# Contrast adjustment on one core: the third and sixth load split into 58 and 6 KB of each row, and the first and fourth store made to wait for GpSimd

## The chip, the core and the metric

The kernel runs on one core of a Trainium2 chip. The names of the profile are used for its engines: PE is TensorE (matrix multiplies), DVE is VectorE, ACT is ScalarE, POOL is GpSimd, and SP is the engine whose queue starts the transfers (DMA) between the chip's main memory (HBM) and the on-chip buffer (SBUF). The SBUF has 128 partitions; an array of 128x16384 is 16384 numbers in each of them. A started transfer is carried out by 16 DMA engines side by side. The metric is the device time of one execution in microseconds (us).

## What is computed

The input `x` holds 16 images of 3 channels, 512x512 float32 numbers each: 48 planes of 262144 pixels, 50.33 MB. The factor is 1.5.

```python
mean = np.mean(x, axis=(2, 3), keepdims=True)
return np.clip(mean + factor * (x - mean), 0, 1).astype(np.float32)
```

A plane can't be written before all of it has been read, since its mean needs every pixel. Every byte is read once and written once, 100.66 MB in all.

## The kernel before, in words

The kernel sees `x` as one line of numbers and cuts it into six tiles of 128 rows with 16384 numbers (64 KB) each, 8 planes to a tile, 16 rows to a plane. A tile is 8.39 MB. The buffer `ring` has three slots, so tile `t` uses slot `t % 3`: tiles 0, 1 and 2 come in at once, and tiles 3, 4 and 5 can be loaded only when the stores of tiles 0, 1 and 2 have emptied their slots.

All transfers are started by SP (`load`, line 77; `store`, line 80), in the order in which the program text names them, and SP does not go past one that still waits. That order, written out at the end of the kernel, is: tile 0 in three loads (2048, 6144 and 8192 columns), load 1, load 2, the stores of tile 0, 1 and 2, loads 3, 4 and 5, the stores of tile 3, 4 and 5.

`compute(t)` does the following to a tile once it has landed:

- The row sums. DVE adds up the first 4352 columns (`tensor_reduce`, line 85) and ACT the others, by a copy of them onto themselves that also writes their sum (line 89). Tile 0 is done in two halves of 8192 columns. The partial sums go into columns of `sums`.
- The mean. PE multiplies each partial sum by the constant `blockw`, which adds up the 16 rows of a plane and scales the result; the products are accumulated in `bias`, in PSUM (line 100).
- The pixels. DVE makes two passes over the tile in place: multiply by the factor and add the bias (line 103), then clip to 0 and 1 (line 106).
- The store. Tile 0 is done in two cuts: columns 0 to 2048 get both passes and a store of 1 MB, then the other 14336 columns get theirs and a store of 7 MB. All other tiles are one cut.

POOL only prepares constants and `blockw` at the start (lines 61 and 63). The waits between engines and transfers are put in by the framework from what each instruction reads and writes; the order on each engine is that of the text.

Of the kernel before, what the change touches and what calls it, by code (L numbers as in the profile page):

```python
# [1 line left out]

# [4 lines left out]


P = 128  # L10
ROW = 16384
HALF = ROW // 2
BUFS = 3
SHORT = 2048
SUM = 4352


@with_exitstack
def kernel(
    ctx: ExitStack,  # L20
    tc: tile.TileContext,
    x: bass.AP,
    factor: float,
    out: bass.AP,
):

    nc = tc.nc
    f32 = mybir.dt.float32  # L30
    Alu = mybir.AluOpType
    Act = mybir.ActivationFunctionType

    B, C, H, W = x.shape
    n_img, n_pix = B * C, H * W
    ppi = n_pix // ROW
    per_tile = P // ppi
    n_tiles = n_img // per_tile
    assert ppi * ROW == n_pix and per_tile * n_tiles == n_img

    factor = float(factor)
    wconst = (1.0 - factor) / float(n_pix)

    x_f = x.rearrange("b c h w -> (b c h w)")
    out_f = out.rearrange("b c h w -> (b c h w)")

    def dram(ap, t, c0=0, c1=ROW):
        return bass.AP(tensor=ap.tensor, offset=t * P * ROW + c0, ap=[[ROW, P], [1, c1 - c0]])

    consts = ctx.enter_context(tc.tile_pool(name="consts", bufs=1))  # L50
    xpool = ctx.enter_context(tc.tile_pool(name="xpool", bufs=1))
    small = ctx.enter_context(tc.tile_pool(name="small", bufs=1))
    psum = ctx.enter_context(tc.tile_pool(name="psum", bufs=1, space=bass.MemoryType.PSUM))


    sums = small.tile([P, 4 * n_tiles], f32, name="sums")
    bias = psum.tile([P, n_tiles], f32, name="bias")

    blockw = consts.tile([P, P], f32, name="blockw")
    blocks = blockw.rearrange("p (a b) -> p a b", b=ppi)  # L60
    nc.gpsimd.memset(blockw, wconst)  # L61
    for base, step in ((0, -ppi), (ppi - 1, ppi)):
        nc.gpsimd.affine_select(  # L63
            out=blocks,
            in_=blocks,
            compare_op=Alu.is_ge,
            fill=0.0,
            base=base,
            pattern=[[step, per_tile], [0, ppi]],
            channel_multiplier=1 if step < 0 else -1,  # L70
        )


    ring = xpool.tile([P, BUFS, ROW], f32, name="ring")

    def load(t, c0=0, c1=ROW):
        nc.sync.dma_start(out=ring[:, t % BUFS, c0:c1], in_=dram(x_f, t, c0, c1))  # L77

    def store(t, c0=0, c1=ROW):
        nc.sync.dma_start(out=dram(out_f, t, c0, c1), in_=ring[:, t % BUFS, c0:c1])  # L80

    def add(t, col, c0, c1, c2):
        xt = ring[:, t % BUFS, :]
        own = sums[:, 4 * t + col : 4 * t + col + 2]
        nc.vector.tensor_reduce(  # L85
            out=own[:, 0:1], in_=xt[:, c0:c1], axis=mybir.AxisListType.X, op=Alu.add
        )
        part = xt[:, c1:c2]
        nc.scalar.activation(out=part, in_=part, func=Act.Copy, accum_out=own[:, 1:2])  # L89
        return [own[:, 1:2], own[:, 0:1]]  # L90

    def compute(t, *cuts):
        xt = ring[:, t % BUFS, :]
        if t == 0:
            parts = add(t, 0, 0, SUM, HALF) + add(t, 2, HALF, HALF + SUM, ROW)
        else:
            parts = add(t, 0, 0, SUM, ROW)
        shift = bias[:, t : t + 1]
        for k, part in enumerate(parts):
            nc.tensor.matmul(shift, blockw, part, start=k == 0, stop=k == len(parts) - 1)  # L100
        for c0, c1 in zip((0, *cuts), (*cuts, ROW)):
            part = xt[:, c0:c1]
            nc.vector.tensor_scalar(  # L103
                out=part, in0=part, scalar1=factor, scalar2=shift, op0=Alu.mult, op1=Alu.add
            )
            nc.vector.tensor_scalar(  # L106
                out=part, in0=part, scalar1=0.0, scalar2=1.0, op0=Alu.max, op1=Alu.min
            )
            store(t, c0, c1)

    with tc.manual_schedule():
        load(0, 0, SHORT)
        load(0, SHORT, HALF)
        load(0, HALF, ROW)
        load(1)
        load(2)
        compute(0, SHORT)
        compute(1)
        compute(2)
        load(3)  # L120
        load(4)
        load(5)
        compute(3)
        compute(4)
        compute(5)


# [1 line left out]
_INS = ['x', 'factor']  # L129
_OUTS = [((16, 3, 512, 512), 'float32')]  # L130

_NUMBERS = {'factor': 1.5}


# [26 lines left out]
```

## Time and profile before

| what | value |
|---|---|
| time, median of 3 runs (lowest, highest) | 239.5 us (239.36, 239.76) |
| profiled execution, first to last instruction (span) | 237.3 us |
| bytes moved, mean rate over the span | 100.66 MB, 424 GB/s |
| DVE busy / ACT busy / POOL busy | 137.4 / 59.9 / 1.1 us |

The profiled execution is one run of its own, and its record gives the span only; no time of its own that would take in what lies around the span. The median of the runs is 2.2 us above that span.

In the timeline each row gives the start of an instruction in us from the start of the span, its duration, the engine, the line of the kernel, the operation, what it writes and reads, how many are merged in the row, and in brackets how long the engine sat idle before and what ended that. A table by stretches of time gives for each stretch the busy time of each engine and, in the last two columns, the mean busy share of the 16 DMA engines and the rate at which they moved bytes; a packet is counted where it starts, so a share can exceed 1. The rows of the DMA queue are its packets, their bytes, and the time that they took as a share of 16 engines' span.

### The profile page before, as it was taken

To read this page: it belongs to the slowest core of one execution; us is meant where nothing else is said; L and a number is where in the kernel's file an instruction comes from. 1 tells how busy PE (TensorE), PEld (TensorE's weight loads), DVE (VectorE), ACT (ScalarE), POOL (GpSimd) and SP (SyncE) were. 2 spreads that over 40 slices of the span, in tenths; PEclk is the share of its full clock that TensorE was granted. 3 is DMA by queue.
4 is the path that set the end of the run, shared out by engine and by line. 5 is a ranking of instruction groups with operands and counts; after the bars stand their busy time and mean duration, and the time that the engine had idled before them with its cause. 6 is when DMAs were issued, how large, how long until landed. Compare 5 with 4: busy or idle time off the path is not lost.

```text
span 237.3 us, 186 instructions
## 1 busy us (share of the span) xinstructions
PE 7.9 (3%) x28; PEld 6.9 (3%) x28; DVE 137.4 (58%) x21; ACT 59.9 (25%) x15; POOL 1.1 (0%) x7
## 2 busy tenths in 40 slices
PE   0010100010001000000000000100000000000000
PEld 0010100010001000000000000100000000000000
DVE  0071899949998998000000043499989998991000
ACT  2051300980492000000000049319509800000000
POOL 1000000000000000000000000000000000000000
DMA  7999989899799798989899998989899998989894
GB/s 289 418 442 442 530 353 530 353 486 398 331 464 454 341 530 353 530 353 519 365 442 442 398 486 353 530 354 530 353 475 409 431 453 376 508 353 530 353 530 177
DMA packets 2160, 100.66 MB, mean 424 GB/s; under 512 B 240, under 2 KB 240, under 8 KB 240
## 3 DMA queue, kind: packets, MB, share of 16 engines
q1 hardware_dynamic: 2160, 100.66, 98.7%
HBM read 50.33 MB, written 50.33 MB: 424 GB/s over the span
## 4 chain that ended last, share of the span: by engine, by line
DVE 43%; DMA 36%; ACT 9%; PE 2%; SPq 1%; issue 0%; DVEq 0%; ACTq 0%
DMA ring<-in_x_dram 36%; DVE ring L103 18%; DVE ring L106 18%; ACT ring L89 9%; DVE sums L85 6%; PE bias L100 2%; SPq L77 1%; SPq L80 0%; DVEq L103 0%; ACTq L89 0%
## 5 line engine op out<-in xcount | busy, mean ns | idle before, releaser
L89 ACT ACTIVATE ring<-ring 128x12032 f32<-128x12032 f32 (+1 forms) x7 | 58.0, 8280 | 128.2 <-DMA ring<-in_x_dram 128.2
L85 DVE TENSOR_REDUCE sums<-ring 128x1 f32<-128x4352 f32 x7 | 32.8, 4683 | 63.9 <-DMA ring<-in_x_dram 63.9
L103 DVE TENSOR_SCALAR ring<-ring,bias 128x16384 f32<-128x16384 f32 (+2 forms) x7 | 52.8, 7538 | 12.9 <-PE bias L100 12.9
L106 DVE TENSOR_SCALAR ring<-ring 128x16384 f32<-128x16384 f32 (+2 forms) x7 | 52.3, 7476 | 0.2
L100 PE MATMUL bias<-sums,blockw 128*128 128x1 f32 x28 | 7.9, 360 | 189.1 <-ACT ring L89 175.4
L100 PEld LDWEIGHTS bias<-sums,blockw 128*128 128x128 f32 x28 | 6.9, 314 | 190.0 <-ACT ring L89 159.4
L89 ACT ACT_TABLE_LOAD x1 | 1.3, 1283 | 0.8 <-PEq L142 0.8
L89 ACT ACTIVATION_READ_ACCUMULATOR ring<-ring 128x1 f32 x7 | 1.3, 187 | 0.0
L63 POOL TENSOR_SCALAR_AFFINE_SELECT blockw<-blockw 128x128 f32<-128x128 f32 x2 | 0.7, 340 | 0.1
L61 POOL MEMSET blockw<- 128x128 f32 x1 | 0.2, 204 | 0.3 <-POOLq L142 0.3
L142 POOL MEMSET const-bfloat16-1.0<- 128x1 bf16 x1 | 0.1, 102 | 0.0
L142 POOL MEMSET const-uint8-127<- 128x1 uint8 x1 | 0.1, 102 | 0.0
L142 POOL MEMSET const-float32-0.0<- 128x1 f32 x1 | 0.1, 98 | 0.3 <-issue 0.3
L142 POOL MEMSET const-float32-1.0<- 128x1 f32 x1 | 0.1, 98 | 0.0
## 6 DMA issues: line engine op xcount, KB each, us to landing
out_dram<-ring SPq DMA_DIRECT2D x1, 7168.0 KB, 35.9
ring<-in_x_dram SPq DMA_DIRECT2D x1, 4096.0 KB, 20.8
ring<-in_x_dram SPq DMA_DIRECT2D x1, 3072.0 KB, 11.6
ring<-in_x_dram SPq DMA_DIRECT2D x1, 1024.0 KB, 4.7
out_dram<-ring SPq DMA_DIRECT2D x1, 1024.0 KB, 34.3
ring<-in_x_dram SPq DMA_DIRECT2D x5, 57.7
out_dram<-ring SPq DMA_DIRECT2D x5, 27.0
```

Of the source, the lines that this page charges most:

```text
L61: nc.gpsimd.memset(blockw, wconst)
L63: nc.gpsimd.affine_select(out=blocks, in_=blocks, compare_op=Alu.is_ge, fill=0.0, base=base, pattern=[[step, per_tile], [0, ppi]], channel ...
L77: nc.sync.dma_start(out=ring[:, t % BUFS, c0:c1], in_=dram(x_f, t, c0, c1))
L85: nc.vector.tensor_reduce(out=own[:, 0:1], in_=xt[:, c0:c1], axis=mybir.AxisListType.X, op=Alu.add)
L89: nc.scalar.activation(out=part, in_=part, func=Act.Copy, accum_out=own[:, 1:2])
L100: nc.tensor.matmul(shift, blockw, part, start=k == 0, stop=k == len(parts) - 1)
L103: nc.vector.tensor_scalar(out=part, in0=part, scalar1=factor, scalar2=shift, op0=Alu.mult, op1=Alu.add)
L106: nc.vector.tensor_scalar(out=part, in0=part, scalar1=0.0, scalar2=1.0, op0=Alu.max, op1=Alu.min)
L142: nc = _bacc.Bacc("TRN2", target_bir_lowering=False, num_devices=1)
```

## The change

Tiles 2 and 5 come in by two loads each: columns 0 to 14848 (58 KB of each row), then the last 1536 columns (6 KB). The cut of tile 0 is gone; it gets one pass of each kind and one store, like the others. Tiles 0 and 3 have the last 32 columns clipped by POOL instead of DVE. Just ahead of that clip POOL copies column 0 of tile 2 (of tile 5) into a column of `sums`; this copy needs the 58 KB part of that tile. DVE's sum of that tile starts at column 1, and the copied column goes to PE as a third partial sum. Since the store of tile 0 (tile 3) needs the columns that POOL clips, it waits for POOL, and so for the 58 KB part.

```diff
+TAIL = 1536
+EDGE = 32
+TURNS = {2: 0, 5: 3}
...
+    def edge(t):
+        xt = ring[:, t % BUFS, :]
+        own = sums[:, 4 * t + 2 : 4 * t + 3]
+        nc.gpsimd.tensor_copy(out=own, in_=xt[:, 0:1])
+        before = ring[:, TURNS[t] % BUFS, ROW - EDGE : ROW]
+        nc.gpsimd.tensor_scalar(
+            out=before, in0=before, scalar1=0.0, scalar2=1.0, op0=Alu.max, op1=Alu.min
+        )
+        return own
...
+        elif t in TURNS:
+            parts = add(t, 0, 1, SUM, ROW) + [edges[t]]
...
-        for c0, c1 in zip((0, *cuts), (*cuts, ROW)):
-            part = xt[:, c0:c1]
-            nc.vector.tensor_scalar(
-                out=part, in0=part, scalar1=factor, scalar2=shift, op0=Alu.mult, op1=Alu.add
-            )
-            nc.vector.tensor_scalar(
-                out=part, in0=part, scalar1=0.0, scalar2=1.0, op0=Alu.max, op1=Alu.min
-            )
-            store(t, c0, c1)
+        nc.vector.tensor_scalar(
+            out=xt, in0=xt, scalar1=factor, scalar2=shift, op0=Alu.mult, op1=Alu.add
+        )
+        own = xt[:, 0 : ROW - EDGE] if t in TURNS.values() else xt
+        nc.vector.tensor_scalar(
+            out=own, in0=own, scalar1=0.0, scalar2=1.0, op0=Alu.max, op1=Alu.min
+        )
+        for later, turn in TURNS.items():
+            if turn == t:
+                edges[later] = edge(later)
+        store(t)
+
+    def load_split(t):
+        load(t, 0, ROW - TAIL)
+        load(t, ROW - TAIL, ROW)
...
-        load(2)
-        compute(0, SHORT)
+        load_split(2)
+        compute(0)
...
-        load(5)
+        load_split(5)
```

More of the change, by code (lines that the diff above doesn't have):

```diff
@@ L90, in add, with compute @@
         return [own[:, 1:2], own[:, 0:1]]
-    def compute(t, *cuts):
+    def edge(t):
[7 more added lines that the diff above has]
+        return own
+    edges = {}
+    def compute(t):
         xt = ring[:, t % BUFS, :]
```

## The prediction

> **What bounds the kernel now.** I read the busy times first, then the row of the DMA queue.
>
> ```profile
> PE 7.9 (3%) x28; PEld 6.9 (3%) x28; DVE 137.4 (58%) x21; ACT 59.9 (25%) x15; POOL 1.1 (0%) x7
> ...
> q1 hardware_dynamic: 2160, 100.66, 98.7%
> ```
>
> No engine is busy for more than 58% of the span, but the 16 DMA engines are for 98.7%. The transfers are the bound, back to back, from 1.8 us to the end. The direction turns three times: loads 0 to 2, stores 0 to 2, loads 3 to 5, stores 3 to 5. There is no slack in this chain: any stretch in which the DMA engines have nothing queued is added to the time in full, and only packets that take longer than they must can be won back.
>
> So next I looked for slow packets. In the packet records every 64 KB row takes 2.418 us on its DMA engine, reading or writing, with two places as exceptions: the last row of load 2 on each engine (mean 3.53 us, started about 58.1) and the last row of load 5 (mean 2.54). Both are the last reads ahead of stores that were already queued. The timeline shows the first one without packets, by when ACT could start on each landed tile:
>
> ```profile
> 22.58 3.40 ACT L89 ACTIVATE ring<-ring 128x3840 f32<-128x3840 f32 x1 [6.22 <-DMA ring<-in_x_dram]
> ...
> 41.93 10.23 ACT L89 ACTIVATE ring<-ring 128x12032 f32<-128x12032 f32 x1 [15.86 <-DMA ring<-in_x_dram]
> ...
> 62.40 10.23 ACT L89 ACTIVATE ring<-ring 128x12032 f32<-128x12032 f32 x1 [10.15 <-DMA ring<-in_x_dram]
> ...
> 159.21 10.23 ACT L89 ACTIVATE ring<-ring 128x12032 f32<-128x12032 f32 x1 [8.96 <-DMA ring<-in_x_dram]
> ...
> 178.57 10.23 ACT L89 ACTIVATE ring<-ring 128x12032 f32<-128x12032 f32 x1 [9.04 <-DMA ring<-in_x_dram]
> ```
>
> Load 1 came 41.93 - 22.58 = 19.35 us after load 0, load 2 20.47 us after that, load 5 19.36 us after load 4. All that can be won is therefore 3.53 - 2.42 = 1.11 us at the first turn and 0.12 us at the second, 1.2 us or 0.5%.
>
> **The change part by part.** *One store of tile 0 for two.* Eight packets of 8 KB (0.309 us) and eight of 56 KB (2.116) become eight of 64 KB (2.418): 19.40 - 19.34 = 0.06 us won, in the DMA chain. DVE's two passes over 16384 columns (8.76 + 8.70) replace 1.29 + 1.23 + 7.68 + 7.63: 0.4 us less, hidden, because line 103 of tile 1 waits for ACT's sum, which ends at 52.3.
>
> *The split loads.* From packet sizes (24 KB 0.912 us, 56 KB 2.116) a row of 58 KB costs 2.19 us and one of 6 KB 0.23, 0.01 more a row than a whole one: 0.06 us a tile, plus 0.01 for a completion. The second issue on SP (0.4 us) stands behind running transfers. On each DMA engine 8 x 0.234 = 1.87 us of reading remain behind the 58 KB part: this is the cover under which the store must get ready.
>
> *The third matmul* of tiles 2 and 5 is one of about 0.3 us on PE, and DVE's and ACT's sums barely change; the stores of these tiles are ready long before their turn (store 5 at 214.6, started after the stores of 3 and 4). Nothing.
>
> *The wait of the stores.* This decides. SP holds store 0 until POOL is done, and behind it stand stores 1 and 2 and loads 3 to 5; with load 2 through, the DMA engines have nothing else. Without the slow row load 2's 58 KB part has landed everywhere at about 41.91 + 8 x 2.191 = 59.45; load 5's at 159.12 + 17.54 = 176.66 (landings of loads 1 and 4). From POOL's end on, the store costs 0.06 us until SP issues it and 1.02 us until bytes move:
>
> ```profile
> 93.76 0.02 SPq L80
> 93.78 0.04 issue
> ```
>
> SP's first issue was at 0.80, and the table by stretches has its first packets after 1.80:
>
> ```profile
> 1.60:1.80 0.20, 0.00 (x0) 0.00 (x0) 0.00 (x0) 0.20 (x1) 0.20 (x1) 1.00 0.00 0
> 1.80:2.00 0.20, 0.00 (x0) 0.00 (x0) 0.00 (x0) 0.20 (x1) 0.02 (x1) 1.00 2.52 369
> ```
>
> *When does POOL run?* Its own rows are short, but all stand before 1.82 us, with DVE idle until 12.94:
>
> ```profile
> 0.41 0.10 POOL L142 MEMSET const-uint8-127<- 128x1 uint8 x1
> 0.80 0.20 POOL L61 MEMSET blockw<- 128x128 f32 x1 [0.29 <-POOLq L142]
> 1.07 0.75 POOL L63 TENSOR_SCALAR_AFFINE_SELECT blockw<-blockw 128x128 f32<-128x128 f32 x2
> ```
>
> At both turns DVE is in the middle of its passes:
>
> ```profile
> 53.43 8.76 DVE L103 TENSOR_SCALAR ring<-ring,bias 128x16384 f32<-128x16384 f32 x1 [3.07 <-PE bias L100]
> 62.22 8.70 DVE L106 TENSOR_SCALAR ring<-ring 128x16384 f32<-128x16384 f32 x1
> 70.83 4.68 DVE L85 TENSOR_REDUCE sums<-ring 128x1 f32<-128x4352 f32 x1
> ...
> 174.25 8.76 DVE L103 TENSOR_SCALAR ring<-ring,bias 128x16384 f32<-128x16384 f32 x1 [0.75 <-PE bias L100]
> 183.04 8.70 DVE L106 TENSOR_SCALAR ring<-ring 128x16384 f32<-128x16384 f32 x1
> 191.65 4.68 DVE L85 TENSOR_REDUCE sums<-ring 128x1 f32<-128x4352 f32 x1
> ```
>
> The trace has no POOL instruction beside a DVE one, so the wait is bounded from both sides: nothing at the low end, and at the high end until DVE leaves the pair of passes, 70.91 - 59.45 = 11.5 us and 191.74 - 176.66 = 15.1 us. One row speaks for the high end. The sum of line 85 goes through 4352 / 4.68 = 0.93 numbers per ns and partition; the passes, from two widths, (16384 - 2048) / (8.757 - 1.292) = 1.92, and they write as much as they read. [...] I take the high end, with POOL getting in only where a pass ends.
>
> [...] The trace agrees with the doubled rate (1.92 against 0.93); that POOL blocks, nothing here shows yet. [...]
>
> **The sum.** POOL has two instructions. The copy may slip between the passes, at 62.20; by then DVE's next pass is waiting and goes next, and the clip comes at its end (if the copy doesn't slip in, both come there). I allow 0.2 us for the copy and 0.34 for the clip, the rows of `blockw`. First turn: 70.91 + 0.2 + 0.34 + 0.06 + 1.02 = 72.5 us for the first bytes of store 0. Before, the last engine had read load 2 at 62.03 (packet records; the landing followed 0.35 us later), and the store went on at once: +10.5 us. Second turn: 191.74 + 0.2 + 0.34 + 0.06 + 1.02 = 193.4 against 178.13: +15.2 us (the second half of the kernel keeps its own clock, counted from load 3). The slow rows and the dearer split vanish in these gaps; the merged store gives 0.06 back. The span becomes 237.3 + 10.5 + 15.2 - 0.1 = 262.9. The runs lie 2.2 us above the span (239.5 against 237.3), which I keep: **265.1 us**. Both terms hang on DVE's rows alone; with POOL's two instructions between nothing and 1 us it is 264.0 to 266.0.
>
> **The rivals.** *POOL runs beside DVE (ends faster).* The store is then issued under the cover. First bytes at 59.45 + 0.04 + 0.2 + 0.34 + 1.08 = 61.1, load 2's data ends at 59.45 - 0.35 + 1.87 = 60.97: a gap of 0.1, and -0.9 against 62.03. Second turn: 178.3 against 178.13, +0.2. With the merged store -0.8: 238.7 us. With POOL's rows at 0.1 each there is no gap: 238.4. A store that starts from empty may pay at each turn what the first loads paid (8 KB packets of 0.6 to 1.0 us instead of 0.31), up to 0.7: 240.1. For it speak POOL's short rows; against it the doubled rate. It decides if POOL's copy starts within 1 us of the landing. Chance 0.30.
>
> *Both of POOL's instructions slip in at the first end of a pass (slower, less so).* Clip done at 62.20 + 0.54, first bytes 63.8: +1.8. Second turn: 183.01 + 0.54 + 1.08 = 184.6: +6.5. Together 8.3, 247.7 us. For it: POOL has both instructions in hand while it waits, and the gap between passes (62.20 to 62.22) exists. Against it: DVE's next pass also waits there. Chance 0.18. One turn this way and one as in the forecast gives 239.5 + 17.0 - 0.1 = 256.4 either way; chance 0.08.
>
> *The forecast*, both turns late by the pair of passes: chance 0.44.
>
> **How the numbers follow.** Two signs hold most of the chance. The forecast's own range is 264.0 to 266.0. Leaving out the fast rival would leave out 3 in 10, so the range goes from its low end, 238.4, to 265.8. A change under 0.2% (0.5 us) can't be told from none here. Of the fast rival's 0.30 I give 0.22 to faster, 0.05 to within, 0.03 to slower (it needs most of the start-up price); all other cases are slower: 0.73 together.
>
> **What would show it.** In the changed profile: POOL's copy of 128x1 and clip of 128x32 starting at the end of a line-103 or line-106 pass, or stretched over it (forecast: copy from 62.2 or 70.9, clip after 70.9); DMA slices with no share between about 61 and 72 us and again for some 15 us at the second turn; SP's store 0 waiting for POOL and not DVE. If the last rows of load 2 run at full rate, as I assume, then its 58 KB part lands near 59.5. I am wrong if POOL's two rows stand near 59.6 with their short durations beside a running pass, or if the packets of the turns are slow even with no store queued.

## The result and the profile after

The changed kernel takes 265.03 us (median of 4 runs, 264.93 to 265.32) against 239.63 us before (239.36 to 239.85). The ratio is 1.107, with a 95% interval of 1.105 to 1.109: 25.4 us slower. The forecast was 265.1 us.

The page of the changed kernel gives the same two rows that stood first in the prediction, and its DMA slices (the span in 40 slices of 6.6 us, busy share in tenths):

```profile
PE 8.7 (3%) x32; PEld 7.7 (3%) x32; DVE 137.2 (52%) x19; ACT 59.9 (23%) x15; POOL 27.6 (10%) x11
...
DMA  7999999972379998997989997999603799799977
...
q1 hardware_dynamic: 2304, 100.66, 89.0%
```

DVE and ACT work as long as before; the DMA engines have the same bytes, but their share of the span fell from 98.7% to 89.0%, and two holes stand in the slices. POOL went from 1.1 to 27.6 us with four instructions more. The table by stretches (busy us of PE, PEld, DVE, ACT and POOL, then the clock, DMA share and GB/s) shows the holes with POOL busy through both:

```profile
62.00:72.00 10.00, 0.10 (x1) 0.11 (x1) 9.96 (x3) 9.84 (x2) 9.11 (x2) 1.00 0.05 20
72.00:74.00 2.00, 0.48 (x2) 0.39 (x2) 2.00 (x1) 0.00 (x0) 0.00 (x0) 1.00 1.01 426
...
190.00:203.00 13.00, 0.58 (x2) 0.50 (x2) 12.96 (x3) 10.19 (x2) 12.99 (x2) 1.00 0.00 0
203.00:205.00 2.00, 0.00 (x0) 0.00 (x0) 2.00 (x1) 0.00 (x0) 0.00 (x0) 1.00 1.24 524
```

From the packet records the DMA engines stood idle for 11.3 us at the first turn and 14.8 at the second (means of the 16 engines): 26.1 us, about as much as the span grew (263.3 - 237.3 = 26.0). The timeline gives the reason (L118 and L122 are DVE's two passes, L98 and L100 POOL's copy and clip, L83 the stores):

```profile
53.53 8.76 DVE L118 TENSOR_SCALAR ring<-ring,bias 128x16384 f32<-128x16384 f32 x1 [3.36 <-PE bias L117]
59.62 2.72 POOL L98 COPY sums<-ring 128x1 f32<-128x1 f32 x1 [57.78 <-DMA ring<-in_x_dram]
61.52 10.23 ACT L92 ACTIVATE ring<-ring 128x12032 f32<-128x12032 f32 x1 [9.16 <-DMA ring<-in_x_dram]
62.30 8.81 POOL L100 TENSOR_SCALAR ring<-ring 128x32 f32<-128x32 f32 x1
62.32 8.73 DVE L122 TENSOR_SCALAR ring<-ring 128x16384 f32<-128x16384 f32 x1
70.97 4.67 DVE L88 TENSOR_REDUCE sums<-ring 128x1 f32<-128x4351 f32 x1
71.14 23.56 SPq L83 DMA_DIRECT2D out_dram<-ring  x3
...
185.42 8.76 DVE L118 TENSOR_SCALAR ring<-ring,bias 128x16384 f32<-128x16384 f32 x1 [0.75 <-PE bias L117]
188.03 6.19 POOL L98 COPY sums<-ring 128x1 f32<-128x1 f32 x1 [116.91 <-DMA ring<-in_x_dram]
...
194.18 8.81 POOL L100 TENSOR_SCALAR ring<-ring 128x32 f32<-128x32 f32 x1
194.21 8.72 DVE L122 TENSOR_SCALAR ring<-ring 128x16384 f32<-128x16384 f32 x1
```

The copy of one column begins when the 58 KB part has landed (59.62) and ends with the pass that is running (62.29). The clip of 32 columns begins then and ends with the next pass (71.05). Store 0 goes out at 71.14, though load 2 was complete at 61.5, as ACT's start shows. The second turn repeats it: DVE's passes there end at 194.2 and 202.9.

### The profile page after: what moved, and what is told of

Same layout as the page of the kernel before. It is cut to its first block, busy times and chain, and to the rows that moved or that the text cites. A ratio compares the mean times of both kernels' runs of the same rounds, so it can differ in the third digit from the quotient of the medians.

```text
span 263.3 us, 203 instructions
## 1 busy us (share of the span) xinstructions
PE 8.7 (3%) x32; PEld 7.7 (3%) x32; DVE 137.2 (52%) x19; ACT 59.9 (23%) x15; POOL 27.6 (10%) x11
## 5 line engine op out<-in xcount | busy, mean ns | idle before, releaser
L88 DVE TENSOR_REDUCE sums<-ring 128x1 f32<-128x4352 f32 (+1 forms) x7 | 32.8, 4680 | 74.7 <-DMA ring<-in_x_dram 74.7
L118 DVE TENSOR_SCALAR ring<-ring,bias 128x16384 f32<-128x16384 f32 x6 | 52.5, 8758 | 14.1 <-PE bias L117 14.1
L122 DVE TENSOR_SCALAR ring<-ring 128x16384 f32<-128x16384 f32 (+1 forms) x6 | 52.2, 8698 | 0.2
L98 POOL COPY sums<-ring 128x1 f32<-128x1 f32 x2 | 8.9, 4453 | 174.7 <-DMA ring<-in_x_dram 174.7
L100 POOL TENSOR_SCALAR ring<-ring 128x32 f32<-128x32 f32 x2 | 17.6, 8814 | 0.0
L117 PE MATMUL bias<-sums,blockw 128*128 128x1 f32 x32 | 8.7, 359 | 199.9 <-ACT ring L92 185.4
L117 PEld LDWEIGHTS bias<-sums,blockw 128*128 128x128 f32 x32 | 7.7, 316 | 200.8 <-ACT ring L92 169.3
```

What stands on the lines that cost most here:

```text
L88: nc.vector.tensor_reduce(out=own[:, 0:1], in_=xt[:, c0:c1], axis=mybir.AxisListType.X, op=Alu.add)
L98: nc.gpsimd.tensor_copy(out=own, in_=xt[:, 0:1])
L100: nc.gpsimd.tensor_scalar(out=before, in0=before, scalar1=0.0, scalar2=1.0, op0=Alu.max, op1=Alu.min)
L118: nc.vector.tensor_scalar(out=xt, in0=xt, scalar1=factor, scalar2=shift, op0=Alu.mult, op1=Alu.add)
L122: nc.vector.tensor_scalar(out=own, in0=own, scalar1=0.0, scalar2=1.0, op0=Alu.max, op1=Alu.min)
```

## The experiments

The theory: POOL stands still while DVE runs a pass at the doubled rate (1.92 numbers per ns and partition, against 0.93 in its sums). The rivals: the wait for a part of a load costs the time whichever engine sees it; any DVE work holds POOL; POOL waits for DVE by a semaphore of the program; POOL's two instructions are slow in themselves.

### ACT in place of POOL

```diff
-        nc.gpsimd.tensor_copy(out=own, in_=xt[:, 0:1])
+        nc.scalar.activation(out=own, in_=xt[:, 0:1], func=Act.Copy)
...
-        nc.gpsimd.tensor_scalar(
-            out=before, in0=before, scalar1=0.0, scalar2=1.0, op0=Alu.max, op1=Alu.min
-        )
+        nc.scalar.activation(out=before, in_=before, func=Act.Copy)
```

(Both stand behind ACT's sum of the tile in between, so that they don't hold it up; DVE clips all columns.)

> The copy of column 0 and the touch of the last 32 columns go from POOL to ACT, which is idle at both turns (DVE clips all columns; ACT copies the last 32 onto themselves). Same wait for the 58 KB part, same two small instructions. My theory (POOL stands still while a DVE pass at the doubled rate runs): ACT does both within 0.6 us of the landing, store 0 is issued near 60.2 and not 71.1, and the time is 238.7 us (238.4 to 240.1). Rival (the wait for a landed part costs the time, whichever engine sees it): 265 us again.

Measured: 239.19 us, ratio 0.9987 (0.9978 to 0.9997). The timeline of this run:

```profile
59.56 0.20 ACT L98 ACTIVATE sums<-ring 128x1 f32<-128x1 f32 x1 [7.23 <-DMA ring<-in_x_dram]
59.67 0.21 ACT L100 ACTIVATE ring<-ring 128x32 f32<-128x32 f32 x1
59.91 34.73 SPq L83 DMA_DIRECT2D out_dram<-ring  x3
```

The wait, the split and the order of the transfers are those of the changed kernel, and the 25 us are gone; store 0 is out 11.2 us earlier. So the wait itself costs nothing here. The other half of the expectation failed in size: only 0.17 us were won, where 0.8 had been expected. The slow rows (64 KB rows that take longer than the usual 2.418 us) did not vanish. They went to the next turn: the last rows of store 2, ahead of load 3, took 0.79 us too long (mean of the 16 engines), where before they were on time.

### DVE at the single rate while POOL works

```diff
+        cut = {1: 10000, 4: 3000}.get(t, 0)
+        for c0, c1 in ((0, cut), (cut, cut + 6384), (cut + 6384, ROW)) if cut else ((0, ROW),):
...
+            if cut and c0 == cut:
+                nc.vector.scalar_tensor_tensor(
+                    out=part, in0=part, scalar=factor, in1=shift.to_broadcast([P, c1 - c0]),
+                    op0=Alu.mult, op1=Alu.add,
+                )
```

> POOL keeps both instructions. Only the 6384 columns of the multiply-and-add pass that DVE works on when the 58 KB part lands (tiles 1 and 4) go through scalar_tensor_tensor, which I expect to run at the single rate (6384 / 0.93 = 6.9 us instead of 3.3); DVE reads and writes the SBUF all the same. My theory (the doubled rate shuts POOL out): POOL's copy and clip are short beside that instruction, store 0 issued near 60.3, time 238.7 us (238.4 to 240.2). Rivals: any DVE work on the SBUF shuts POOL out: POOL waits to the end of that instruction (65.5 at the first turn) or of the pass behind it, 243 us or more; POOL waits for DVE by a semaphore that the program has and not by the rate: the end of the passes, 265 us or a little more.

The timeline:

```profile
58.80 6.79 DVE L122 SCALAR_TENSOR_TENSOR ring<-ring,bias 128x6384 f32<-128x6384 f32 x1
59.60 0.18 POOL L98 COPY sums<-ring 128x1 f32<-128x1 f32 x1 [57.77 <-DMA ring<-in_x_dram]
59.74 0.31 POOL L100 TENSOR_SCALAR ring<-ring 128x32 f32<-128x32 f32 x1
60.09 37.89 SPq L83 DMA_DIRECT2D out_dram<-ring  x3
```

DVE's instruction runs at 6384 / 6.79 = 0.94 numbers per ns, reads and writes the SBUF throughout, and POOL's two instructions inside it take 0.18 and 0.31 us. "Any DVE work" and "slow in themselves" are out, and so is a semaphore: what the two instructions depend on was not touched. One thing is not separated: every doubled-rate instruction in these runs is a `tensor_scalar`, and every single-rate one another operation, so no run tells the rate itself from something else that goes with `tensor_scalar`. The time was 241.94 us (ratio 1.010, 1.009 to 1.012) and not 238.7, for a reason that I had not reckoned: DVE is 3.4 us later behind the first turn and 4.0 behind the second, and the last store, whose pass ends at 218.6, came too late for the DMA engines, which were done with store 4 before:

```profile
217.00:219.00 2.00, 0.00 (x0) 0.00 (x0) 1.60 (x1) 0.00 (x0) 0.00 (x0) 1.00 0.00 0
```

That hole is 2.4 us in the packet records. Without it the run would be at about 239.5 us (an estimate, 241.94 - 2.4).

### The other condition: POOL's turn while DVE idles or sums

```diff
-TAIL = 1536
+TAIL = 8192
```

> The split is 32 and 32 KB of each row, so the first part lands near 51.7, when DVE is idle (50.2 to 53.5), and at the second turn near the start of DVE's line-88 sum (single rate). My theory: POOL's two instructions take 0.1 to 0.4 us each at both turns, beside the sum too, the stores are queued some 9 us before the loads end, and no gap is left: 239.6 us if the last rows of load 2 are slow again behind a queued store, 238.4 if not. Rival (POOL's copy or clip is slow by itself on these operands, 2.7 and 8.8 us as in the changed kernel): POOL ends near 63, 241 to 243 us. Rival (the wait costs, not POOL): a gap at each turn stays, over 245 us.

Measured: 239.33 us, ratio 0.9994 (0.9985 to 1.0003). POOL's rows are 0.18 and 0.32 us at both turns, at the first in a pause of DVE, at the second beside its sum:

```profile
51.68 0.18 POOL L98 COPY sums<-ring 128x1 f32<-128x1 f32 x1 [49.85 <-DMA ring<-in_x_dram]
51.83 0.32 POOL L100 TENSOR_SCALAR ring<-ring 128x32 f32<-128x32 f32 x1
...
168.83 4.68 DVE L88 TENSOR_REDUCE sums<-ring 128x1 f32<-128x4352 f32 x1
169.04 0.18 POOL L98 COPY sums<-ring 128x1 f32<-128x1 f32 x1 [116.89 <-DVE ring L122]
169.18 0.32 POOL L100 TENSOR_SCALAR ring<-ring 128x32 f32<-128x32 f32 x1
```

The store was then queued 10 us ahead of load 2's end (52.17, against ACT's start on the tile at 62.49), and the slow rows were back at the first turn (1.09 us), as in the kernel before.

### One turn alone

```diff
-TURNS = {2: 0, 5: 3}
+TURNS = {2: 0}
...
-        load_split(5)
+        load(5)
```

> Only the first turn has the split load and the wait for POOL; tile 5 comes in one load and store 3 waits for DVE alone. My theory: the first term of the sum alone, a gap of 11.2 us as in the changed kernel, less what the queued store of before cost there: 249.6 to 251.0 us. Rival (one of the turns does all the harm): 239 or 265 us.

Measured: 251.28 us in one execution, 0.3 above the range. The gap is 11.2 us as expected, and the slow rows came twice, 0.7 us ahead of load 3 and 1.1 us ahead of store 3.

### Pieces, and one instruction in place of two

How does POOL get in between passes? First, the passes that it meets are cut in eight:

```diff
+        step = 2048 if t in (1, 4) else ROW
+        for c0 in range(0, ROW, step):
+            part = xt[:, c0 : c0 + step]
...
```

> POOL keeps both instructions; the multiply-and-add pass of tiles 1 and 4 is cut into eight pieces of 2048 columns, 1.3 us each, at the doubled rate as before. My theory, with the hold ending with each instruction and POOL getting one instruction in at each end: copy done at the first end (near 60.1), clip at the next (near 61.4), first bytes of store 0 near 62.3; at the second turn some 1 us late; time 240.8 us (240.0 to 242.0). Rival (POOL waits by a semaphore for the whole of DVE's passes of that tile): 265 us. Rival (the hold lasts while DVE has pieces in its queue, back to back): 265 us too, and POOL's rows tell the two apart by where they start.

Measured: 245.59 us, ratio 1.025 (1.023 to 1.027), with gaps of 3.2 and 3.3 us; neither 240.8 nor 265. The timeline:

```profile
53.33 9.69 DVE L121 TENSOR_SCALAR ring<-ring,bias 128x2048 f32<-128x2048 f32 x8 [3.27 <-PE bias L117]
59.63 1.03 POOL L98 COPY sums<-ring 128x1 f32<-128x1 f32 x1 [57.80 <-DMA ring<-in_x_dram]
60.63 2.45 POOL L100 TENSOR_SCALAR ring<-ring 128x32 f32<-128x32 f32 x1
```

The copy ends with the piece that it met, so the hold does not last while DVE has more pieces queued. The clip lasts over two pieces and not one, at both turns. So "one instruction at each end" is wrong for the clip. The next run gave POOL a single instruction, on 32 columns:

```diff
-        nc.gpsimd.tensor_copy(out=own, in_=xt[:, 0:1])
...
-            out=before, in0=before, scalar1=0.0, scalar2=1.0, op0=Alu.max, op1=Alu.min
+            out=before, in0=before, scalar1=xt[:, 0:1], scalar2=xt[:, 0:1], op0=Alu.subtract, op1=Alu.add
```

> POOL has one instruction at each turn in place of two: it takes column 0 of the later tile off the last 32 columns of the earlier one and adds it again (a change by rounding only), so it sees the 58 KB part and touches what the store needs; DVE clips all columns and adds up from column 0. My theory with one POOL instruction at each end of a pass: it ends at the end of the line-118 pass (62.3, and 183.0 on the clock of before), the store is out at once, gaps of some 2.2 and 5.8 us: 247.3 us. Rival (POOL needs two ends of passes for an instruction on 32 columns, or waits for the pair by a semaphore): 265 us. Rival (the two-instruction chain is not the point, POOL slips in whole): 239 us.

Measured: 265.09 us, ratio 1.107 (1.105 to 1.108), like the changed kernel. One instruction stood through the end of one pass and the whole of the next:

```profile
59.73 11.31 POOL L98 TENSOR_SCALAR ring<-ring 128x32 f32<-128x32 f32 x1 [57.90 <-DMA ring<-in_x_dram]
...
62.24 8.74 DVE L118 TENSOR_SCALAR ring<-ring 128x16384 f32<-128x16384 f32 x1
```

So the end at 62.2 does not let in just any instruction. (No run shows how long this form takes when nothing holds it.) Two runs looked at what gets in, with rows of POOL instructions on scratch tiles that nothing waits for:

```diff
+            nc.gpsimd.tensor_copy(out=probe[:, 0:1], in_=parts[0])
+            for _ in range(40):
+                nc.gpsimd.tensor_scalar(
+                    out=probe, in0=probe, scalar1=0.0, scalar2=1.0, op0=Alu.max, op1=Alu.min
+                )
```

> The kernel before, with a row of 40 small POOL instructions (clip of a 128x32 scratch tile onto itself; its values go nowhere) that starts when ACT's sum of tile 1 is there (52.1), and with the multiply-and-add pass of tile 1 in eight pieces of 2048 columns. No transfer waits for POOL. My theory: POOL gets a fixed small number of steps at each end of a doubled-rate instruction and runs freely beside the line-85 sum. From the run with pieces (copy over one end, clip over two): about one clip for every two pieces, 2.4 us each, then one that lasts over the clip pass of DVE (8.7 us), and 0.15 to 0.35 us each from 71 us on. DVE's pieces are not longer than 1.3 us each, since POOL only uses the moment between them. Time within 0.3 us of before. [...]

Measured: 239.66 us in one execution (239.49 for the kernel before, also one). The rows of the clips (count, least / median / longest ns, first and last start), first beside DVE's pieces, then beside its sum:

```profile
L106 POOL TENSOR_SCALAR probe<-probe x3: 2317/2317/2320, 54.8 to 59.6; 128x32 f32<-128x32 f32 x3
```

```profile
L106 POOL TENSOR_SCALAR probe<-probe x11: 313/313/315, 72.0 to 76.0; 128x32 f32<-128x32 f32 x11
```

The same instruction takes 0.31 us beside a sum at the single rate and 2.32 us, two pieces less the time between two clips, beside pieces at the doubled rate; over the clip pass of DVE one took 8.64 us. The first and the last clip beside the pieces needed one end only (1.35 and 1.23 us). DVE's eight pieces took 9.71 us together, against 9.69 in the run with pieces above, with hardly a POOL instruction beside them:

```profile
53.30 9.71 DVE L114 TENSOR_SCALAR ring<-ring,bias 128x2048 f32<-128x2048 f32 x8 [3.00 <-PE bias L100]
```

So POOL waits, and DVE hardly does.

The other run had eight of another form at each of four tiles:

> The kernel before with the multiply-and-add passes of tiles 1, 2, 4 and 5 in eight pieces of 2048 columns, and beside each a row of eight POOL instructions of one form on a scratch tile whose values go nowhere: writes only (memset of 32 columns) at tile 1, copies of 32 columns at tile 2, copies of 1 column at tile 4, clips of 1 column at tile 5. No transfer waits for POOL. The run with 40 clips had most of its clips of 32 columns take two pieces, and DVE's pieces not lengthened. If reading and writing each need an end of a piece of their own: writes only take one piece (1.2 us), all others two (2.4 us). If what counts is the number of columns: one column takes one piece, 32 columns two, the writes of 32 too. If writes alone are not held: 0.1 to 0.2 us for them. Time within 0.5 us of before.

Measured: 240.09 us in one execution (239.93 for the kernel before, also one). Beside the pieces, copies of 32 columns (the one of 213 ns had begun before the first piece), copies of one and clips of one:

```profile
L109 POOL COPY probe<-probe x7: 213/1139/1139, 77.0 to 83.2; 128x32 f32<-128x32 f32 x7
```

```profile
L111 POOL COPY probe<-probe x6: 1139/1139/1142, 174.6 to 180.6; 128x1 f32<-128x1 f32 x6
```

```profile
L113 POOL TENSOR_SCALAR probe<-probe x6: 1057/1117/1119, 198.4 to 204.3; 128x1 f32<-128x1 f32 x6
```

One piece each; the writes (memset) took 1.08 and 1.14 us, one piece too. All three guesses fail: reading and writing need no end each, the number of columns alone doesn't decide, and writes alone are held too. What the rows share is their length when nothing holds them: forms of 0.12 to 0.21 us needed one end, the clip of 32 columns with 0.31 us mostly two. Why the length should decide, no run shows. DVE's clip pass differs a little with it: it took 8.73 us in the changed kernel and 8.74 with the single POOL instruction on 32 columns, where POOL was not done when the pass began, against 8.69 in the next run, where it was. The last run put the short forms to use, with a single short instruction (it replaces the last column of the output of tiles 0 and 3 by input):

```diff
-        before = ring[:, TURNS[t] % BUFS, ROW - EDGE : ROW]
...
+        before = ring[:, TURNS[t] % BUFS, ROW - 1 : ROW]
+        nc.gpsimd.tensor_copy(out=before, in_=xt[:, 0:1])
```

> POOL has one instruction at each turn, and one of the short forms: it copies column 0 of the later tile over the last column of the earlier one (that column of the output of tiles 0 and 3 is replaced by input; DVE clips and sums everything else as before). Theory as the runs left it (a POOL instruction that takes 0.2 us alone gets in at the first end of a pass): copy done at 62.3 and 194.2 less the shift of the first turn, stores out at once, first bytes near 63.2 against 61.05 and near 184 against 178.2 on the clock of before: gaps of 2.2 and 5.9 us, 247.2 us (246.5 to 248). Rival (a POOL instruction that arrives in the middle of a pass needs the ends of both passes of the pair, as the one with two pointers did): 265 us.

Measured: 247.60 us, ratio 1.0325 (1.031 to 1.034), 0.4 us from the expectation; gaps of 2.3 and 6.1 us.

```profile
60.17 2.21 POOL L98 COPY ring<-ring 128x1 f32<-128x1 f32 x1 [58.34 <-DMA ring<-in_x_dram]
62.37 8.69 DVE L116 TENSOR_SCALAR ring<-ring 128x16384 f32<-128x16384 f32 x1
62.41 31.99 SPq L83 DMA_DIRECT2D out_dram<-ring  x3
```

What matters between this run and the changed kernel is whether POOL is through at the first end of a pass or at the second: 17.4 us.

### The slow rows

> The kernel before with tile 0 in one cut: one store of 64 KB rows in place of 8 KB and 56 KB rows. No split load, no wait. The slow last row of load 2 (1.11 us too long) is the question. If the short rows queued behind it made it slow: row back to 2.42 to 2.5 us, 238.4 us. If any queued store does, once a run: the slow row stays, 239.3 us (only the 0.06 us of the shorter store).

```diff
-        compute(0, SHORT)
+        compute(0)
```

Measured: 239.41 us, ratio 1.0005 (0.999 to 1.002). The slow rows of load 2 stayed (1.18 us), and those of load 5 took 0.4 us too long, against 0.1 before. So the short rows queued behind them are not the cause, and the merged store is worth nothing that can be measured. Then all three turns were held back with ACT:

```diff
+        if t == 2:
+            store(t, 0, ROW - TAIL)
+            store(t, ROW - TAIL, ROW)
+            for slot in (2, 0):
+                spot = ring[:, slot, 0:1]
+                nc.scalar.activation(out=spot, in_=spot, func=Act.Copy)
```

> As the run with ACT in place of POOL, and the turn from stores to loads is held back too: store 2 in 58 and 6 KB of each row, ACT copies a column of slot 2 and of slot 0 onto itself once the 58 KB part is out, and load 3 waits for that. In the ACT run the slow rows went from the first turn to this one (0.79 us). If rows are slow because transfers of the other direction are queued behind them, none are slow now: 238.4 to 238.8 us. If the delay is something that comes once a run at the first turn with no gap, it goes on to the next turn or into the gaps: 239.2 us.

Measured: 239.84 us, ratio 1.0018 (1.0009 to 1.0027): 0.4 us above before, and no gain. Gaps of 0.1, 0.4 and 0.4 us came at the turns, and the first rows of load 3, with nothing of the other direction queued behind, still took 0.7 us too long.

## Why the prediction was right, point by point

- **The bound** was read rightly: no slack, so the 26.1 us in which the DMA engines stood idle came out as the growth of the span (26.0).
- **The doubled rate as a sign that POOL is shut out**, the step on which everything hung: shown for DVE's `tensor_scalar` passes, the only doubled-rate work here. The same two POOL instructions take 2.7 and 8.8 us beside a doubled-rate pass, 0.18 and 0.31 us beside DVE work at the single rate in the same place; one clip takes 2.32 us beside doubled-rate pieces and 0.31 beside a `tensor_reduce`. The step from the rate to a wait of POOL was my estimate. What holds POOL no run shows; the rows show how long it is held, to 71.1 and 203.0 at the two turns of the changed kernel.
- **The copy at the first end, the clip at the second**: right in the rows, but my reason was not the right one. I had one instruction get in at each end. A single one on 32 columns needed both ends just the same (265.1 us), and a single short one only the first (247.6). The rival in which POOL is through at the first end was priced at 247.7; a kernel in which it holds measured 247.6.
- **First turn**: forecast +10.5, measured +10.2 (store 0 landed at 91.92 against 81.75). POOL's instructions cost 0.06 us past the end of the pass in place of 0.54, and the first packets came 0.85 us after SP's issue in place of 1.02.
- **Second turn**: forecast +15.2, measured +14.8 (end against the landing of load 5), for the same reason.
- **Slow rows vanish**: wrong. They were gone at the two held turns and came back between them, 0.85 us at the turn from stores to loads, and the rows of the stores were a little longer. Between the landings of store 0 and load 3 the shift grew from 10.2 to 11.2 us. This term of 1 us I had at nothing; it covered the two terms that I had too large, 10.2 + 1.0 + 14.8 = 26.0 against 10.5 + 15.2 - 0.1 = 25.6.
- **The agreement to 0.1 us** is luck. The sum put the span at 262.9 us, 0.4 below the measured 263.3. The step from the span to the time was 0.4 too large: the 2.2 us set the median of some executions against the span of another one. Where an execution has both (265.08 and 263.3 here), the time lies about 1.8 us above the span.
- **The range**, 238.4 to 265.8, took in the rivals as well. So the time alone would not bear the forecast out; the rows of POOL and SP do, and they show the case that had a chance of 0.44.
- **The fast rival** had its condition right (an engine that sees the part at once) and its prize too large: 238.7 forecast, 239.2 measured with ACT, since it counted on the slow rows to vanish as well.

## What to carry to other kernels

Before an instruction of a second engine is put into a chain that the DMA queue waits for, compare the rate of what DVE runs at that moment with that of its slowest work: beside DVE work at twice the rate (1.92 numbers per ns against 0.93) POOL got in, in these runs, only where a DVE instruction ended, and a tiny instruction lasted up to 14.9 us (the single instruction on 32 columns at the second turn), the rest of one pass and the whole of the next. The same job on ACT cost nothing here (239.19 us against 239.36 before). And before a delay is chased in a saturated queue, see whether it goes away or only moves: the slow rows at one turn (1.11 us in the kernel before) came back at the next (0.79 with ACT), so that the best of these runs won 0.13% (0.03 to 0.22).

## What was not expected of the hardware

- POOL instructions held off by a row of doubled-rate DVE instructions got in at the ends of these and cost DVE next to nothing (9.71 against 9.69 us for eight pieces, some 0.05 us at most for a pass, 8.74 against 8.69); forms of up to 0.21 us needed one end, a clip of 128x32 (0.31 us when nothing held it) mostly two.
- Rows that took 0.7 to 1.2 us too long, at turns of the transfers between reading and writing: at the first turn in the kernel before (1.11 us), the second in the changed kernel (0.85) and in the ACT run (0.79), the second and third with one turn held back (0.7 and 1.1). They came without short rows behind them (1.18 us too long with one store of tile 0) and without a queue of the other direction (0.7 us with all three turns held back). What makes them slow stays open.
